# Experts of a mixture-of-experts stage worked in pairs: one transpose of the inner rows for two experts, another order of weight loads and products, ScalarE's gate work behind the feature copies

## The chip, the cores and the metric

The kernel runs on one core of one Trainium2 chip. The metric is the device time of one execution in microseconds (us). A kernel's time is the median of its runs.

## The reference, cut to what matters

An encoder of two layers over 512 tokens of width 1024, in float32. Each layer is a mixer (retention and differential attention in the first, latent attention and gated linear attention in the second), a LayerNorm, a mixture of 32 experts, and another LayerNorm. The change lies in the mixture:

```python
def _hier_moe(x, w_grp, b_grp, w_exp, b_exp, w_gate, w_up, w_down):
    ...
    gate = p_grp[:, None] * jax.nn.softmax(top_l, axis=-1)
    ...
    def expert_block(args):
        idx, e = args
        xb = x_pad[idx]
        hdn = jax.nn.silu(xb @ w_gate[e]) * (xb @ w_up[e])
        return hdn @ w_down[e]
    ...
    out = jnp.zeros((n + 1, d), x.dtype).at[buf_tok].add(y * buf_w[:, None].astype(y.dtype))
```

Every token goes to two of the 32 experts, so all experts are used and all their weights are read: per expert and layer w_gate and w_up of 1024 x 512 and w_down of 512 x 1024, 6 MB, 403 MB over both layers.

## The kernel before, in words

**Weights.** A weight slab is 128 x 2048 float32, 1 MB, and an expert has six: gate and up in two halves each, down in two. `expect_moe` lists the loads in the order in which the products use them; SyncE issues them in that order (line 304), each into a free slot (`slot`, `pump`). A slot is free when TensorE has used its slab. `spare` holds slots back for other tiles.

**Products.** Expert `e` holds up to 64 tokens. Two experts `2p` and `2p+1` make pair `p`: their 128 token rows are fetched from DRAM by GpSimd's indirect DMA (`moe_fetch`, line 1174; below "the gather") to places that `moe_pair` works out on TensorE (4 transposes and 4 small products with `G`) and VectorE (`ridx`). `moe_features` turns these rows with 8 transposes into one PSUM tile, and ScalarE copies it to `xn` (line 1185), two buffers by the pair's parity. `up(e, c)` is half `c` of the gate and up products, 8 products of 64 x 512 (16 matmul instructions in the trace), with `xn` as the stationary operand. After the second half `moe_hidden` makes silu(gate) * up on ScalarE and VectorE (lines 1211 and 1212) in the 64 x 512 tile `h`. `hidden(e)` turns it with 4 transposes of 64 rows and a VectorE copy into `hs`. `down(e)` is 8 products; `moe_gated` (lines 1241, 1242) scales its result by the gate. `sums(p, t)` adds a pair's result to token tile `t`: 4 products with `C` and a VectorE addition (line 1197).

**Order.** In `moe` TensorE's order is the program's. For each expert it is `up(e, 1)`, `down(e-1)`, `up(e+1, 0)`, then `hidden(e)`, and between these `pair` or `features` of a later pair and, at every second expert, the four `sums` of the pair before. A pair's features come at least one expert before the products that read them. The other engines' order comes from a scheduler. Before the first expert stand `moe_features` of pair 0 with two copies, and `moe_gates`, which makes the gate values in `G` (exponentials and a cast on ScalarE). At the end follow `sum_begin`, the last `down`, `sum_end` and the LayerNorm.

Of the kernel before, what the change touches and what calls it, by code (L numbers as in the profile page):

```python
# [11 lines left out]
F32 = mybir.dt.float32  # L12
# [4 lines left out]
AF = mybir.ActivationFunctionType  # L17
OP = mybir.AluOpType
AX = mybir.AxisListType

P = 128
D = 1024
# [7 lines left out]
NE = 32  # L30
NG = 4
EPG = 8
DE = 512
CAP = 64
# [41 lines left out]
class Kernel:  # L76
# [220 lines left out]
    def expect_moe(self, l):  # L297

        I = self.I

        def half(n, e, c):
            j = 4 if n == "moe_w_down" else 8
            wv = I[n][l, e].rearrange("(p j) n -> p j n", j=j)
            self.expect(lambda raw: self.nc.sync.dma_start(
                raw.rearrange("p (j n) -> p j n", j=j // 2), wv[:, c * (j // 2):(c + 1) * (j // 2), :]), local=True)

        def up(e, c):
            half("moe_w_gate", e, c)
            half("moe_w_up", e, c)

        up(0, 0), up(0, 1), up(1, 0)
        for e in range(1, NE + 1):
            if e < NE:
                up(e, 1)
            for c in range(2):
                half("moe_w_down", e - 1, c)
            if e + 1 < NE:
                up(e + 1, 0)

    def new_xT(self):  # L320

# [855 lines left out]
    def moe_features(self, x, xn, parts=1):  # L1177

        xv = x.rearrange("p (k j) -> p j k", j=KJ)
        ps = self.pb()  # L1180
        for j in range(KJ):
            self.tr(ps[:, j * P:(j + 1) * P], xv[:, j, :])
        n = KJ // parts
        for i in range(parts):
            self.nc.scalar.copy(xn[:, i * n:(i + 1) * n], ps[:, i * n * P:(i + 1) * n * P].rearrange("p (j n) -> p j n", j=n))  # L1185
        self.rel(ps)

    def moe_sum(self, m, C, y, ts, first):

# [7 lines left out]
            self.nc.vector.scalar_tensor_tensor(x, x, ALPHA if first else 1.0, ps, op0=OP.mult, op1=OP.add)  # L1197
            self.rel(ps)

    def moe_up(self, o, x, c):  # L1200

        raws = [self.next_raw()[0] for _ in range(2)]
        for j in range(4):
            for i, raw in enumerate(raws):
                self.mm(o[64 * i:64 * i + 64], x[:, 4 * c + j, :], raw[:, j * 512:(j + 1) * 512], c == 0 and j == 0,
                        c == 1 and j == 3)
        self.free(*raws)

    def moe_hidden(self, h, o):

        self.nc.scalar.activation(h, o[0:64], AF.Silu)  # L1211
        self.nc.vector.tensor_tensor(h, o[64:128], h, op=OP.mult)  # L1212
        self.rel(o)

    def moe_hidden_rows(self, r, h):

        hv = h.rearrange("p (k j) -> p j k", j=4)
        ps = self.pa()
        for j in range(4):
            self.tr(ps[:, j * CAP:(j + 1) * CAP], hv[:, j, :], 64)  # L1220
        hs = r.tile([P, 4, CAP], F32, name="hs", bufs=1)
        self.nc.vector.tensor_copy(hs.rearrange("p j n -> p (j n)"), ps[:, 0:4 * CAP])  # L1222
        self.rel(ps)
        return hs

# [20 lines left out]
    def moe(self, m, g, b):  # L1246

        nc, tc, l = self.nc, self.tc, m["layer"]
        self.more_slots(1)
        wst = ExitStack()  # L1250
        r = wst.enter_context(tc.tile_pool(name=f"moe{l}", bufs=1))
        h, C, zs, xs = {}, {}, {}, {}
        LAST = NE // 2 - 1
        hh = r.tile([P, DE], F32, name="h")
        C2 = r.tile([P, 2, T], F32R, name="C")
        m["G"] = r.tile([P, NT, NE // 2, 6], F32R, name="G")
        xbuf, xr, sc = m["xbuf"], m["xr"], m["sc"]
# [2 lines left out]
        def pair(p):  # L1260
            C[p] = last[:, D:D + T] if p == LAST else cz[:, 0:T] if p == LAST - 1 else \
                [sc[:, D:D + T], sc[:, D + T:2 * D], C2[:, 0], C2[:, 1]][p % 4]
            self.moe_pair(m, p, C[p])
            if p + 2 <= LAST:
                self.moe_places(m, p + 2)
            if p > 1:
                self.moe_fetch(m, p)

        def features(p):
            self.moe_features(self.moe_fetched(m, p), xn[:, p % 2])  # L1270

        def parts(t):

            xs[t] = self.slot(F32R)
            self.split(xs[t][:, 0:D], xs[t][:, D:2 * D], self.residual(m, t))
# [27 lines left out]
        y1 = None  # L1303

        def up(e, c):
            if c == 0:
                acc[e] = self.pa()
            self.moe_up(acc[e], xn[:, e // 2 % 2, :, e % 2 * CAP:(e % 2 + 1) * CAP], c)
            if c == 1:
                h[e] = hh[64:128]  # L1310
                self.moe_hidden(h[e], acc.pop(e))

        def hidden(e):
            hs[e] = self.moe_hidden_rows(r, h.pop(e))

        def down(e):
            pd = self.pa() if e < NE - 1 else self.pb()
            for c in range(2):
                self.moe_down(pd, hs[e], c)
            del hs[e]  # L1320
            a, p = 64 * (e % 2), e // 2
            gate = m["gate"][:, p:p + 1]
            if p < LAST:
                z = (yz if p == LAST - 1 else yhl).rearrange("p (k n) -> p k n", k=2)
                self.moe_gated(z[:, 0], z[:, 1], pd, gate, a)
                return
            b_, y1 = 64 - a, last[:, 0:D]
            f, s = slice(b_ * 8, b_ * 8 + 512), slice(a * 8, a * 8 + 512)
            self.after = nc.scalar.activation(y1[a:a + 64, f], pd[b_:b_ + 64, 0:512], AF.Copy, scale=gate[a:a + 64]).ins
            nc.vector.tensor_scalar(y1[a:a + 64, s], pd[a:a + 64, 0:512], gate[a:a + 64], None, op0=OP.mult)  # L1330
            self.rel(pd)

        def sums(p, *ts):
            self.moe_sum(m, C[p], yhl.rearrange("p (k n) -> p k n", k=2), ts, p == 0)

        acc, hs = {}, {}
# [3 lines left out]
        with tc.manual_schedule(engines={mybir.EngineType.PE}):  # L1340
            x = self.moe_fetched(m, 0)
            nc.vector.tensor_copy(x, m["g"])
            self.rel(m.pop("g"))
            self.moe_features(x, xn[:, 0], 2)
            ps = self.pa()
            self.moe_tokens(m, m["S"][:, :, 2:4], self.idr, ps, 1)
            self.rel(ps)
            self.moe_fetch(m, 1, False)
            self.moe_gates(m)
            self.spare = 1  # L1350
            up(0, 0)
            yhl = self.slot(F32R)
            self.spare = 0
            up(0, 1)
            up(1, 0)
            for e in range(NE):
                q, k = divmod(e, 4)
                p = e // 2 - 1
                if e == NE - 10:
                    self.spare = 4  # L1360
                if e == NE - 8:
                    last, cz, yz, gbuf = self.slot(local=False), self.slot(F32R, local=False), self.slot(F32R, local=False), None
                    gbuf = self.load_gb(g, b)
                    self.spare = 0
                    nc.vector.tensor_copy(cz[:, T:T + P], self.eye)
                if e:
                    up(e, 1)
                    down(e - 1)
                    if e + 1 < NE:
                        up(e + 1, 0)  # L1370
                if e == NE - 1:
                    hidden(e)
                    break
                if e == 0:
                    features(1)
                    pair(0), pair(1)
                more = q + 1 < NE // 4
                if k % 2:
                    hidden(e)
                    if more and k == 1:  # L1380
                        pair(2 * q + 3)
                    elif more:
                        features(2 * q + 3)
                    continue
                add = 0 <= p < LAST - 1
                if add:
                    sums(p, 0)
                hidden(e)
                if add:
                    sums(p, 1)  # L1390
                if more and k == 0:
                    pair(2 * q + 2)
                elif more:
                    features(2 * q + 2)
                if add:
                    sums(p, 2, 3)
                if p == LAST - 2:
                    self.spare = 1
                    self.free(sc, yhl)
                    y = yz.rearrange("p (k n) -> p k n", k=2)  # L1400
                    parts(0)
                    self.spare = 2
                if e == NE - 2:
                    self.spare = 0
                    parts(1), parts(2)
            y1 = last[:, 0:D]
            sum_begin(0)
            down(NE - 1)
            sum_begin(1)
            for t in range(3):  # L1410
                sum_end(t)
                if t == 0:
                    sum_begin(2)
# [555 lines left out]
```

## Time and profile before

| | |
|---|---|
| median of 3 runs | 1535.87 us (1528.81, 1535.87, 1539.55) |
| the profiled execution | 1532.13 us; its span from first to last instruction 1530.4 us |
| mean granted clock of TensorE | 0.993 of full speed |
| busy in the span | TensorE 96%, VectorE 47%, ScalarE 28%, GpSimd 9% |
| weight slabs of the experts | 384 loads of 1024 KB, median 18.4 to 19.6 us from issue to landing |
| HBM | 462.11 MB read, 308 GB/s over the span |

The two expert stages lie at about 325 to 785 us and 1050 to 1515 us. A busy TensorE in the profile is not one at its peak, since matmuls are pipelined and their ends are modelled; so pieces of work are measured here from the start of one group of matmuls to the start of the next. In a row, "idle before <- releaser" in square brackets is how long the engine stood before the group and what ended it.

### The profile page before, as it was taken

What the parts mean: (1) busy time and instruction counts of PE and PEld (TensorE: products, weight loads), DVE (VectorE), ACT (ScalarE), POOL (GpSimd) and SP (SyncE); (2) the same over time, 40 slices, a digit from 0 to 9 for tenths busy, and PEclk for the clock granted to TensorE, in tenths of its full rate; (3) what the DMA queues carried; (4) which work ended last, traced back from release to release, by engine and by line L of the source; (5) the groups of instructions that cost most, each with busy time, mean ns of one, the idle gap of its engine ahead of it and who ended that gap; (6) DMA issues with size and microseconds to landing.
All of it is one profiled execution on the core that took longest, in us unless ns stands there. A gap on an engine that the chain in (4) does not pass through costs nothing. (4 is left out here: it accounts for less than half of the span.)

```text
span 1530.4 us, 18251 instructions
## 1 busy us (share of the span) xinstructions
PE 1474.0 (96%) x7057; PEld 840.0 (55%) x7057; DVE 722.6 (47%) x1336; ACT 432.9 (28%) x817; POOL 137.1 (9%) x194
## 2 busy tenths in 40 slices
PE   7999999989999999999999999998999999999997
PEld 6777787854444444444357777684444444444433
DVE  5766858553343343343355744473334334334334
ACT  4655421022112112112246545402221211211222
POOL 0211101120000000010021000111000000001001
PEclk9999999999999999999999999998999999999999
DMA  8211314789999999999962210587999999999993
GB/s 263 65 56 56 108 65 159 270 326 424 426 427 425 426 426 427 425 426 426 427 211 99 83 55 28 209 344 272 407 426 427 425 427 425 427 425 426 426 427 134
DMA packets 105119, 465.02 MB, mean 304 GB/s; under 512 B 13308, under 2 KB 44508, under 8 KB 55744
## 3 DMA queue, kind: packets, MB, share of 16 engines
q1 hardware_dynamic: 97136, 444.86, 71.6%
q0 software_dynamic: 6160, 12.62, 2.4%
q10 hardware_dynamic: 1728, 6.29, 1.0%
q8 instruction: 57, 0.93, 0.2%
q14 instruction: 38, 0.31, 0.1%
HBM read 462.11 MB, written 9.44 MB: 308 GB/s over the span
## 5 line engine op out<-in xcount | busy, mean ns | idle before, releaser
L211 PE MATMUL pa<-big 128*64 128x512 f32 (+2 forms) x3400 | 813.8, 521 | 11.1 <-DMA big<-in_moe_w_up_dram 3.1
L211 PEld LDWEIGHTS pa<-big 128*64 128x64 f32 (+1 forms) x3400 | 397.1, 158 | 345.2 <-issue 272.9
L211 PE MATMUL pa<-big,hs 128*64 128x512 f32 x992 | 224.8, 592 | 0.0
L1242 DVE SCALAR_TENSOR_TENSOR big<-pa,rgate,big 64x512 fp32r<-64x512 f32 x120 | 90.0, 750 | 213.4 <-ACT big L1241 210.5
L211 PE MATMUL pb<-big 128*128 128x512 f32 (+1 forms) x544 | 159.8, 431 | 8.3 <-DVE big L1197 4.2
L1197 DVE SCALAR_TENSOR_TENSOR big<-big,pb 128x1024 f32<-128x1024 f32 x112 | 134.3, 1220 | 69.4 <-PE pb L211 69.1
L211 PEld LDWEIGHTS pa<-big,hs 128*64 128x64 f32 x992 | 72.9, 137 | 140.6 <-issue 134.5
L1212 DVE TENSOR_TENSOR h<-pa,h 64x512 f32<-64x512 f32 x64 | 44.4, 694 | 219.7 <-ACT h L1211 219.7
L1241 ACT ACTIVATE big<-pa,rgate 64x512 fp32r<-64x512 f32 x120 | 81.9, 683 | 218.9 <-PE pa L211 170.2
L211 PEld LDWEIGHTS pb<-big 128*128 128x128 f32 x544 | 98.0, 190 | 54.2 <-issue 25.8
L1211 ACT ACTIVATE h<-pa 64x512 f32<-64x512 f32 x64 | 37.7, 590 | 262.0 <-PE pa L211 262.0
L201 DVE TENSOR_TENSOR big<-big 128x1024 fp32r<-128x1024 f32 (+2 forms) x67 | 80.0, 1207 | 31.6 <-ACT big L201 25.8
L201 ACT CAST big<-big 128x1024 fp32r<-128x1024 f32 (+2 forms) x68 | 68.9, 1044 | 56.0 <-PE pa L211 37.2
L1185 ACT COPY big<-pb 128x1024 f32<-128x1024 f32 (+1 forms) x34 | 32.5, 962 | 118.7 <-PE pb L216 118.7
L1174 POOL DMA_INDIRECT big<-x1d,ridx x30 | 31.4, 1048 | 353.6 <-DVE ridx L1148 232.7
L211 PE MATMUL pb<-big,C 128*128 128x512 f32 x192 | 53.9, 412 | 2.5 <-DVE big L1197 2.5
L216 PEld LDWEIGHTS pa<-eye,h 64*128 64x128 f32 x256 | 35.5, 209 | 37.9 <-DVE big L1242 24.3
L1173 POOL MEMSET big<- 128x1024 f32 x28 | 26.7, 953 | 325.4 <-PE pb L216 325.4
L216 PE MATMUL pb<-eye,big 128*128 128x128 f32 x304 | 43.0, 286 | 8.0 <-DMA big<-in_x_dram 5.0
L1222 DVE COPY hs<-pa 128x256 f32<-128x256 f32 x64 | 27.0, 422 | 43.6 <-PE pa L216 43.5
L216 PEld LDWEIGHTS pb<-eye,big 128*128 128x128 f32 x304 | 38.9, 194 | 14.1 <-issue 11.1
L216 PE MATMUL pa<-eye,h 64*128 64x64 f32 x256 | 44.2, 293 | 0.0
(313 smaller groups left out, 1164.3 us busy)
## 6 DMA issues: line engine op xcount, KB each, us to landing
big<-in_moe_w_gate_dram SPq DMA_DIRECT2D x128, 1024.0 KB, 18.4
big<-in_moe_w_up_dram SPq DMA_DIRECT2D x128, 1024.0 KB, 19.6
big<-in_moe_w_down_dram SPq DMA_DIRECT2D x128, 1024.0 KB, 19.6
big<-in_ev_w_in_dram SPq DMA_DIRECT2D x32, 256.0 KB, 4.8
big<-in_ev_w_in_dram SPq DMA_DIRECT2D x12, 512.0 KB, 5.8
big<-in_od_w_in_dram SPq DMA_DIRECT2D x6, 1024.0 KB, 5.5
big<-in_x_dram SPq DMA_DIRECT2D x8, 512.0 KB, 6.8
big<-in_ev_w_out_dram SPq DMA_DIRECT2D x4, 1024.0 KB, 5.1
```

Source lines behind the costliest of these rows:

```text
L201: ins = self.nc.scalar.copy(hi, src), (sub or self.nc.vector).tensor_tensor(lo, src, hi.bitcast(F32), op=OP.subtract)
L211: return self.nc.tensor.matmul(o, a, b, start=start, stop=stop, skip_group_check=True)
L216: self.nc.tensor.transpose(o, a, self.eye[s, s])
L1173: self.nc.gpsimd.memset(x, 0.0)
L1174: self.nc.gpsimd.indirect_dma_start(x, None, self.x1d[:, :], bass.IndirectOffsetOnAxis(m["idx"][:, pair:pair + 1], 0), bounds_check=T - 1, ...
L1185: self.nc.scalar.copy(xn[:, i * n:(i + 1) * n], ps[:, i * n * P:(i + 1) * n * P].rearrange("p (j n) -> p j n", j=n))
L1197: self.nc.vector.scalar_tensor_tensor(x, x, ALPHA if first else 1.0, ps, op0=OP.mult, op1=OP.add)
L1211: self.nc.scalar.activation(h, o[0:64], AF.Silu)
L1212: self.nc.vector.tensor_tensor(h, o[64:128], h, op=OP.mult)
L1222: self.nc.vector.tensor_copy(hs.rearrange("p j n -> p (j n)"), ps[:, 0:4 * CAP])
L1241: last = self.nc.scalar.activation(hi, src, AF.Copy, scale=g[a:a + 64])
L1242: self.nc.vector.scalar_tensor_tensor(yl[a:a + 64, s], src, g[a:a + 64], hi.bitcast(F32), op0=OP.mult, op1=OP.subtract)
```

## The change

It does five things.
- Loads and products go by pairs: all four halves `up(e+2, ..)`, `up(e+3, ..)` of the next pair lie around the two `down` of this pair, and `expect_moe` lists the slabs in that order.
- The inner rows of both experts stand in one 128 x 512 tile (the free end of the router's tile `y1`, in the place of `h`), and one `hidden(p)` per pair makes 4 transposes of 128 rows and one copy of 512 columns. The odd expert's gate and up halves of PSUM change places for that.
- `features(p + 2)` stands at the end of pair `p`, after `up(e+3, 1)` and straight before `up` of the pair that reads it. `pair(p + 2)` stands after `down(e)`.
- The four `sums` come as two and two, on either side of `up(e+2, 1)`.
- `moe_gates` is issued after the copies of the first features on ScalarE. At the end `hidden` of the last pair and its two `down` follow `sum_begin(0)`.

As `y1` is now in use through the first layer's experts, the loads of the second layer's router weights into a tile of the same place stand behind the last gather in GpSimd's order; before, they stood behind the second.

```diff
-        up(0, 0), up(0, 1), up(1, 0)
-        for e in range(1, NE + 1):
...
+        for e in range(2):
+            up(e, 0), up(e, 1)
+        for e in range(0, NE, 2):
+            if e + 2 < NE:
+                up(e + 2, 0), up(e + 2, 1)
+            for k in range(2):
+                for c in range(2):
+                    half("moe_w_down", e + k, c)
+                if e + 2 < NE:
+                    up(e + 3, k)
...
-    def moe_up(self, o, x, c):
+    def moe_up(self, o, x, c, a):
...
-                self.mm(o[64 * i:64 * i + 64], x[:, 4 * c + j, :], raw[:, j * 512:(j + 1) * 512], c == 0 and j == 0,
+                b = 64 - a if i == 0 else a
+                self.mm(o[b:b + 64], x[:, 4 * c + j, :], raw[:, j * 512:(j + 1) * 512], c == 0 and j == 0,
...
-            self.tr(ps[:, j * CAP:(j + 1) * CAP], hv[:, j, :], 64)
-        hs = r.tile([P, 4, CAP], F32, name="hs", bufs=1)
-        self.nc.vector.tensor_copy(hs.rearrange("p j n -> p (j n)"), ps[:, 0:4 * CAP])
+            self.tr(ps[:, j * P:(j + 1) * P], hv[:, j, :])
+        hs = r.tile([P, 4, P], F32, name="hs", bufs=1)
+        self.nc.vector.tensor_copy(hs.rearrange("p j n -> p (j n)"), ps)
...
-        hh = r.tile([P, DE], F32, name="h")
+        hh = m["y1"][:, D - DE:D]
...
-            self.moe_gates(m)
+            with tc.issue_after(ins):
+                self.moe_gates(m)
...
+            up(1, 0), up(1, 1)
+            features(1)
+            for p in range(LAST):
+                e = 2 * p
...
+                up(e + 2, 0)
+                hidden(p)
+                if p:
+                    sums(p - 1, 0, 1)
+                else:
+                    pair(0)
+                up(e + 2, 1)
+                if p:
+                    sums(p - 1, 2, 3)
...
+                down(e)
+                if p == 0:
+                    pair(1)
+                if p + 2 <= LAST:
+                    pair(p + 2)
+                up(e + 3, 0)
+                down(e + 1)
+                up(e + 3, 1)
+                if p + 2 <= LAST:
+                    features(p + 2)
...
             sum_begin(0)
+            hidden(LAST)
+            down(NE - 2)
             down(NE - 1)
```

TensorE's order in the middle of the first stage, before: `pa<-big` of 64x512 is an `up` half, `pa<-big,hs` a `down`, `pa<-eye,h` the transposes of `hidden`, `pb<-big,C` the `sums`, `pb<-eye,big` the features, `pa<-eye,big` and `pa<-G,big` a `pair`.

```order
L211 MATMUL pa<-big 64x512 x8
L216 MATMUL pa<-eye,h 128x64 x4
L216 MATMUL pa<-eye,big 128x128 x4
L211 MATMUL pa<-G,big 128x6 x4
L211 MATMUL pa<-big 64x512 x8
L211 MATMUL pa<-big,hs 64x512 x8
L211 MATMUL pa<-big 64x512 x8
L211 MATMUL pb<-big,C 128x512 x4
L216 MATMUL pa<-eye,h 128x64 x4
L211 MATMUL pb<-big,C 128x512 x4
L216 MATMUL pb<-eye,big 128x128 x8
L211 MATMUL pb<-big,C 128x512 x8
```

The same engine and place in the changed kernel, a whole pair from features to features, where `pa<-eye,y_111` is the one `hidden` of the pair:

```order
L216 MATMUL pb<-eye,big 128x128 x8
L211 MATMUL pa<-big 64x512 x8
L216 MATMUL pa<-eye,y_111 128x128 x4
L211 MATMUL pb<-big,C 128x512 x8
L211 MATMUL pa<-big 64x512 x8
L211 MATMUL pb<-big,C 128x512 x8
L211 MATMUL pa<-big,hs 64x512 x8
L216 MATMUL pa<-eye,big 128x128 x4
L211 MATMUL pa<-G,big 128x6 x4
L211 MATMUL pa<-big 64x512 x8
L211 MATMUL pa<-big,hs 64x512 x8
L211 MATMUL pa<-big 64x512 x8
```

The features moved to the place just ahead of the `up` half that reads them, and one `hidden` is gone.

TensorE at the end of the second stage, before, from the last `up` half to the last `down` (`pb<-big,hs`), where `pa<-big` of 128x512 is `sum_begin(0)`:

```order
L211 MATMUL pa<-big 64x512 x8
L211 MATMUL pa<-big,hs 64x512 x8
L216 MATMUL pa<-eye,h 128x64 x4
L211 MATMUL pa<-big 128x512 x8
L211 MATMUL pb<-big,hs 64x512 x8
```

The same place in the changed kernel (`y_5143` is the second layer's `y1`):

```order
L211 MATMUL pa<-big 64x512 x8
L211 MATMUL pa<-big 128x512 x8
L216 MATMUL pa<-eye,y_5143 128x128 x4
L211 MATMUL pa<-big,hs 64x512 x8
L211 MATMUL pb<-big,hs 64x512 x8
```

The `sum_begin(0)` that stood between the transposes of `hidden` and a `down` now stands ahead of both.

## Rows read from the trace of the kernel before

**Rows 1.** Busy times in one stretch: PE, PEld, DVE, ACT, POOL, clock, DMA share, GB/s.

```profile
336.00:770.00 434.00, 428.67 (x2057) 189.22 (x2057) 163.89 (x243) 86.17 (x124) 28.15 (x29) 1.00 1.01 425
```

**Rows 2.** TensorE in order of time near the first stage's end: start, us, group.

```profile
730.82 1.02 PE L211 MATMUL pa<-big 128*64 128x512 f32 x2
732.12 3.65 PE L211 MATMUL pa<-big 128*64 128x512 f32 x14 [0.28 <-DMA big<-in_moe_w_up_dram]
...
759.08 1.05 PE L211 MATMUL pa<-big 128*64 128x512 f32 x2
761.54 3.65 PE L211 MATMUL pa<-big 128*64 128x512 f32 x14 [1.42 <-DMA big<-in_moe_w_up_dram]
```

**Rows 3.** TensorE's waits from 320 us on: total us, times, longest.

```profile
PE pb L211 <- DVE big L1197: 6.7, 16, 0.4
PE pa L211 <- DMA big<-in_moe_w_up_dram: 3.1, 3, 1.4
```

**Rows 4.** TensorE in order of time, two experts in the first stage.

```profile
512.05 3.65 PE L211 MATMUL pa<-big 128*64 128x512 f32 x16
515.54 3.60 PE L211 MATMUL pa<-big,hs 128*64 128x512 f32 x16
518.97 3.60 PE L211 MATMUL pa<-big 128*64 128x512 f32 x16
522.50 0.69 PE L216 MATMUL pa<-eye,h 64*128 64x64 f32 x4
...
524.06 3.65 PE L211 MATMUL pa<-big 128*64 128x512 f32 x16
...
534.51 1.20 PE L211 MATMUL pb<-big,C 128*128 128x512 f32 x4
535.64 0.69 PE L216 MATMUL pa<-eye,h 64*128 64x64 f32 x4
536.25 1.20 PE L211 MATMUL pb<-big,C 128*128 128x512 f32 x4
537.29 1.05 PE L216 MATMUL pb<-eye,big 128*128 128x128 f32 x8
538.77 2.10 PE L211 MATMUL pb<-big,C 128*128 128x512 f32 x8 [0.42 <-DVE big L1197]
540.80 3.65 PE L211 MATMUL pa<-big 128*64 128x512 f32 x16
```

**Rows 5.** All engines in order of time, first features of the first stage.

```profile
323.97 1.14 PE L216 MATMUL pb<-eye,big 128*128 128x128 f32 x8 [1.47 <-DVEq L1338]
...
325.14 1.07 ACT L1185 COPY big<-pb 128x512 f32<-128x512 f32 x2 [0.64 <-PE pb L216]
...
325.78 10.59 PE L211 MATMUL pa<-big 128*64 128x512 f32 x48 [0.33 <-ACT big L1185]
```

**Rows 6.** Groups by line, 330 to 775 us: busy us, mean ns of one, idle before.

```profile
L1185 ACT COPY big<-pb 128x1024 f32<-128x1024 f32 x15 | 15.2, 1013 | 59.0 <-PE pb L216 59.0
L1222 DVE COPY hs<-pa 128x256 f32<-128x256 f32 x32 | 13.5, 422 | 21.8 <-PE pa L216 21.8
```

**Rows 7.** A gather in order of time.

```profile
525.09 1.04 POOL L1174 DMA_INDIRECT big<-x1d,ridx  x1 [12.56 <-issue]
```

**Rows 8.** The line of the gathers (L1174): time from issue to landing, all 30.

```profile
DMA to landing us min/median/max: 3.4/8.2/9.3
```

**Rows 9.** All engines in order of time, first features of the second stage.

```profile
1047.13 1.14 PE L216 MATMUL pb<-eye,big 128*128 128x128 f32 x8 [1.47 <-DVEq L1338]
...
1049.61 0.30 ACT L201 CAST G<-y 128x128 fp32r<-128x128 f32 x1 [1.95 <-DVE ridx L1148]
1049.81 1.07 ACT L1185 COPY big<-pb 128x512 f32<-128x512 f32 x2
...
1050.44 13.02 PE L211 MATMUL pa<-big 128*64 128x512 f32 x48 [1.84 <-ACT big L1185]
```

**Rows 10.** What the DMA engines moved, GB/s in 40 slices of 1 us from 1040 us.

```profile
GB/s 418 426 229 16 0 33 82 221 377 344 33 41 123 0 0 16 0 82 213 410 377 164 279 442 410 434 426 434 410 434 434 361 221 164 336 369 418 418 410 434
```

More of the change, by code (lines that the diff above doesn't have):

```diff
@@ L309, in up @@
             half("moe_w_up", e, c)
-        up(0, 0), up(0, 1), up(1, 0)
-        for e in range(1, NE + 1):
[L313 to L318, printed above, removed]
+        for e in range(2):
[8 more added lines that the diff above has]
+                    up(e + 3, k)
     def new_xT(self):
@@ L1184, in moe_features @@
         for i in range(parts):
-            self.nc.scalar.copy(xn[:, i * n:(i + 1) * n], ps[:, i * n * P:(i + 1) * n * P].rearrange("p (j n) -> p j n", j=n))
+            ins = self.nc.scalar.copy(xn[:, i * n:(i + 1) * n], ps[:, i * n * P:(i + 1) * n * P].rearrange("p (j n) -> p j n", j=n)).ins
         self.rel(ps)
+        return ins
     def moe_sum(self, m, C, y, ts, first):
@@ L1204, in moe_up, with moe_hidden @@
             for i, raw in enumerate(raws):
-                self.mm(o[64 * i:64 * i + 64], x[:, 4 * c + j, :], raw[:, j * 512:(j + 1) * 512], c == 0 and j == 0,
+                b = 64 - a if i == 0 else a
+                self.mm(o[b:b + 64], x[:, 4 * c + j, :], raw[:, j * 512:(j + 1) * 512], c == 0 and j == 0,
                         c == 1 and j == 3)
         self.free(*raws)
-    def moe_hidden(self, h, o):
-        self.nc.scalar.activation(h, o[0:64], AF.Silu)
-        self.nc.vector.tensor_tensor(h, o[64:128], h, op=OP.mult)
+    def moe_hidden(self, h, o, a):
+        h = h[a:a + 64]
+        self.nc.scalar.activation(h, o[64 - a:128 - a], AF.Silu)
+        self.nc.vector.tensor_tensor(h, o[a:a + 64], h, op=OP.mult)
         self.rel(o)
@@ L1307, in up, with hidden @@
                 acc[e] = self.pa()
-            self.moe_up(acc[e], xn[:, e // 2 % 2, :, e % 2 * CAP:(e % 2 + 1) * CAP], c)
+            self.moe_up(acc[e], xn[:, e // 2 % 2, :, e % 2 * CAP:(e % 2 + 1) * CAP], c, e % 2 * CAP)
             if c == 1:
[L1310 to L1314, printed above, removed]
+                self.moe_hidden(hh, acc.pop(e), e % 2 * CAP)
+        def hidden(p):
+            hs[p] = self.moe_hidden_rows(r, hh)
         def down(e):
+            a, p = 64 * (e % 2), e // 2
             pd = self.pa() if e < NE - 1 else self.pb()
             for c in range(2):
-                self.moe_down(pd, hs[e], c)
-            del hs[e]
-            a, p = 64 * (e % 2), e // 2
+                self.moe_down(pd, hs[p][:, :, a:a + 64], c)
             gate = m["gate"][:, p:p + 1]
@@ L1343, in moe @@
             self.rel(m.pop("g"))
-            self.moe_features(x, xn[:, 0], 2)
+            ins = self.moe_features(x, xn[:, 0], 2)
             ps = self.pa()
@@ L1354, in moe @@
             up(0, 1)
[L1355 to L1359, printed above, removed]
+            up(1, 0), up(1, 1)
+            features(1)
+            for p in range(LAST):
+                e = 2 * p
+                if p == 11:
                     self.spare = 4
-                if e == NE - 8:
+                if p == 12:
                     last, cz, yz, gbuf = self.slot(local=False), self.slot(F32R, local=False), self.slot(F32R, local=False), None
@@ L1365, in moe @@
                     nc.vector.tensor_copy(cz[:, T:T + P], self.eye)
[L1366 to L1397, printed above, removed]
+                up(e + 2, 0)
[7 more added lines that the diff above has]
+                    sums(p - 1, 2, 3)
+                if p == LAST - 1:
                     self.spare = 1
@@ L1402, in moe @@
                     self.spare = 2
-                if e == NE - 2:
-                    self.spare = 0
-                    parts(1), parts(2)
+                down(e)
[8 more added lines that the diff above has]
+                    features(p + 2)
+            self.spare = 0
+            parts(1), parts(2)
             y1 = last[:, 0:D]
             sum_begin(0)
+            hidden(LAST)
+            down(NE - 2)
             down(NE - 1)
```

## The prediction, made before the changed kernel ran

> **What bounds the kernel now.** I read the page's slices first, then the busy times of the stretch between the first and the last expert, then TensorE in order of time inside it and at its two ends, and last ScalarE and the DMA around the start of each stage. In the stretch the DMA share is 1.01 at 425 GB/s and TensorE is busy 428.67 of 434 us [rows 1], so both look like the bound. TensorE's waits tell them apart. From 320 us to the end it waits for a weight slab only three times, 3.1 us in total [rows 3], and in the first stage only near its end [rows 2]. So for most of the stage TensorE trails the DMA: slabs were loaded ahead while it still worked on the mixer, and it draws nearer all the time. One pair of experts costs it 28.75 us, from 512.05 to 540.80 [rows 4]. The DMA needs 12 slabs of 1.049 MB at 425 GB/s, 29.6 us, and more with the gather. TensorE therefore gains about 1 us and a half per pair and meets the DMA near 730 us. There two matmuls that take 0.43 us elsewhere (16 in 3.43, from 515.54 to 518.97 [rows 4]) stretch to 1.30 and 2.46 [rows 2], so TensorE loses 0.87 and 2.03 us, together 2.9 us. That is all the slack: TensorE may become 2.9 us slower over a whole stage before the end of the stage moves, and if it becomes faster it only meets the DMA earlier.
>
> **What each part costs TensorE, over one stage of 16 pairs.**
>
> Inner rows: 32 groups of 4 transposes go, 0.61 us each from 535.64 to 536.25 [rows 4], 19.5 us. 16 groups of 4 transposes of 128 rows come. Eight such transposes take 1.06 us (537.29 to 538.77 less a wait of 0.42 [rows 4]); four are 0.53, with the change of tile shape about 0.55, and no more than the old 0.61. That is 8.8 us. Gain 10.7.
>
> Sums: two blocks of 4 and one of 8 cost 1.13, 1.04 and 2.03 (534.51 to 535.64, 536.25 to 537.29, 538.77 to 540.80), 4.20; two blocks of 8 cost 4.06. Over 14 pairs this gains 2.0. The wait for VectorE's addition, 0.42 us and 8 times in a stage (16 in both [rows 3]), goes too, since an `up` half of 3.4 us now stands between the two blocks: gain 3.4.
>
> Shape changes: an `up` or `down` in the middle of a run costs 3.43, the first of a run 3.49 and the last 3.53 [rows 4]. Two runs of three become one run of three and three single groups, 0.32 us more per pair, 4.8 in 15.
>
> Features: this is the new wait. Until now a pair's features were an expert ahead; now the `up` that reads them is the next thing in TensorE's order. At the start of the stage the trace shows this very sequence: transposes at 323.97, ScalarE's copy from 325.14, `up` at 325.78, 0.11 after the first half of the copy [rows 5]. In the loop the copy is one piece of 1.013 us [rows 6], so `up` starts 1.17 + 1.01 + 0.11 = 2.29 us after the first transpose instead of 1.06. The stall is 1.23 us, 15 times, 18.4 us. Behind the waiting `up` stand `hidden`, the sums and the next `down`, all in order, so nothing fills it. ScalarE's silu of the expert before needs 0.6 us and is done while the transposes run.
>
> Sum per stage: 18.4 + 4.8 - 10.7 - 2.0 - 3.4 = 7.1 us slower on TensorE. From both sides: were the stall only the copy (1.0) and the four transposes 0.41, it would be 1.3; were the transposes no cheaper and single groups all 0.1 dearer, 10.
>
> End of the stage: the work behind the last `up` half is the same, but `down(30)` now waits for the copy of `hs`. Before, `sum_begin(0)` covered it. The copy of 256 columns takes 0.422 us [rows 6]; 512 columns I put at 0.7, with the way there and back a stall of 0.9 us (0.5 to 1.2).
>
> Start: in the first stage the feature copies follow the transposes at once [rows 5], so moving the gate work gives nothing. In the second stage ScalarE first waits for VectorE with the cast of `G`: the copies start at 1049.81 though the transposes, begun at 1047.13, took 1.14, and TensorE stands 1.84 us [rows 9]. Moved behind, the copies start about 1.5 us earlier. The clock is at 1.2 GHz there after TensorE's pauses (48 matmuls take 13.02 against 10.59 us in the first stage [rows 5, 9]), so 0.8 to 1.5 of it is left; I take 1.1.
>
> DMA: the second stage's DMA stops between 1044 and 1060, and once more it falls, to 221, 164, 336 and 369 GB/s in four slices [rows 10], 1.4 us lost against 426, because no slot came free while TensorE did pairs instead of products. The new order frees eight slabs in one go, and this hole closes. It is worth something only if the DMA sets the end. The router loads that move on GpSimd cost nothing: it is busy 28 of 434 us [rows 1] and their reader is a mixer away; I allow 0 to 2 us for what they take from the DMA at the layer boundary.
>
> **The sum.** First stage 7.1 - 2.9 + 0.9 = 5.1. Second stage, with the same slack (its one large wait is the third of the 3.1 us in rows 3), 5.1 - 1.1 = 4.0. Together 9.1, against the profiled execution's 1532.13: 1541.2. That execution lies 3.7 below the median of the three runs and within their range, so its time is a fair base; I predict 1541.5.
>
> **Rivals.**
>
> *The DMA covers it.* If TensorE's loss stays below the slack, the end hangs on the last slab: 0 in the first stage, -1.1 - 1.4 in the second, plus 0.9 twice for the tails: 1531.4, or 1529.6 if the tails are free. For it speaks the DMA share of 1.01 [rows 1]; against it that TensorE is late for most of the stage and the slack is only 2.9 [rows 2]. It needs a loss of 2.9 or less where I count 7.1 and bound it at 1.3 below. The Trainium skill (Perfetto Trace Analysis, Identifying the Most-Contended Engine) says that gains come from the most contended engine; by it only the DMA would count here and the time would be this rival's. The trace agrees that the DMA is full, but shows TensorE behind it for 400 us.
>
> *Late gather, slower.* The rows of pair p+2 are now asked for in the same pair in which they are transposed. In the trace a gather starts 1.03 us after the next `up` (525.09 and 524.06 [rows 4, 7]). The features follow that `up` after three groups, 10.45 us (512.05 to 522.50 [rows 4]), so it has 9.42 us; it lands after 8.2 in the median and 9.3 at most [rows 8]. That fits by 1.2 and 0.1 us. If `ridx` stands 2.5 us longer on VectorE, behind the additions of `down(e)`, TensorE waits 1.3 us in each of 14 pairs of both stages, 36 us: 1577. It decides once the gather starts 1.2 us later. In the new order `ridx` stands ahead of those additions, which speaks against it.
>
> *The pair's transposes are not cheaper.* If four of 128 rows ran one after another at 0.28 each, `hidden` would cost 1.1 instead of 0.55, 8.8 more per stage: 1558.8. The features' eight in 1.06 us [rows 4] speak against it. The Trainium skill (TensorE: Matmul & The Clock Gate, Part 4: PE-mode transpose) gives about 275 ns for a 128 x 128 transpose inside a kernel, which would make it this; the trace shows 0.13 us each when they follow one another.
>
> **How the numbers follow.** TensorE's loss beyond the slack (forecast) 0.57, the DMA covers it 0.28, late gather 0.10, dear transposes 0.05. The range must leave out no more than 2 in 10: from just under the second case with the runs' own spread, 1528, to beyond the dear transposes, 1562. The forecast alone spans 1533 to 1549. One per cent, about what a measurement of this kernel can tell from no change, is 15.4 us: slower than 1551 are late gather, dear transposes and little else, 0.14; faster than 1520 has no mechanism here but an error of mine, 0.03; within it 0.83.
>
> **What would show it.** In the new profile: a wait of TensorE for ScalarE's feature copy (line 1187) of 1.0 to 1.3 us about 30 times, and a pair of experts at about 29.0 us, waits included; 0.55 us from `hidden` to the next group; no waits for VectorE's additions; the gate cast behind the copies in the second stage and its first products some 1.5 us nearer the transposes; no or smaller waits for slabs near 760 us. If waits for slabs remain at both ends, the DMA covered the loss and I am wrong by the second case. A wait of the features' transposes for a gather would show the third.

## The result and the profile after

The changed kernel takes 1544.85 us (median of 8 runs, 1541.51 to 1550.57), the kernel before 1537.44 in 8 runs beside it: ratio 1.0058, 95% interval 1.0032 to 1.0085. That is 9 us slower by the ratio and 7.4 by the medians, small, though the interval leaves out 1, and within the one per cent that the prediction called "no change". 1541.5 was forecast.

The profiled run took 1541.51 us, the shortest of the eight, its span 1539.7, 9.3 more than before. I read first the busy times of the first stage (columns as in [rows 1]), then TensorE's waits from 320 to 1515 us.

```profile
336.00:780.00 444.00, 424.21 (x2009) 178.99 (x2005) 158.92 (x229) 85.37 (x125) 27.64 (x29) 1.00 1.01 422
```

```profile
PE pa L211 <- ACT big L1187: 33.7, 32, 1.1
PE pa L211 <- DVE big L1247: 4.3, 2, 2.2
...
PE pa L216 <- DVE y L1217: 2.2, 2, 1.1
...
PE pa L211 <- issue: 1.7, 2, 0.8
```

The DMA share is still 1.01, but TensorE is now idle for 19.8 of 444 us where it was idle for 5.3 of 434 [rows 1]. It no longer waits for a slab at all: the row of [rows 3] is gone, and so is VectorE's addition. In its place stands the feature copy, 32 times: 30 in the loop at 1.1 us and one short wait at the start of each stage. Three more come once in a stage: for line 1247 (4.3 us in both stages), for 1217 (2.2) and "issue" (1.7). Only the last was foreseen.

The DMA in 40 slices of 1 us from 1480 us, GB/s:

```profile
GB/s 434 442 426 401 434 451 418 410 418 451 418 410 426 434 410 418 377 385 360 311 180 156 41 0 0 0 0 0 0 0 0 0 0 0 0 0 0 0 0 0
```

The last slab lands at about 1502.5 us; the last `down` of the changed kernel starts at 1512.01. TensorE ends the stage some 9 us behind the DMA. In the kernel before the transfers end as early, and its last `down` starts at 1502.64, level with them:

```profile
GB/s 442 401 426 434 442 426 418 418 418 434 426 418 426 434 410 410 352 377 262 172 123 74 16 0 0 0 0 0 0 0 0 0 0 0 0 397 127 0 0 94
```

TensorE in order of time, one steady pair, answering to [rows 4]:

```profile
517.10 1.17 PE L216 MATMUL pb<-eye,big 128*128 128x128 f32 x8
519.36 3.65 PE L211 MATMUL pa<-big 128*64 128x512 f32 x16 [1.10 <-ACT big L1187]
522.95 0.75 PE L216 MATMUL pa<-eye,y 128*128 128x128 f32 x4
523.45 2.09 PE L211 MATMUL pb<-big 128*128 128x512 f32 x8
...
548.32 1.08 PE L211 MATMUL pa<-big 128*64 128x512 f32 x4 [1.10 <-ACT big L1187]
```

A pair takes 28.96 us (519.36 to 548.32; forecast about 29.0, before 28.75). The pair's `hidden` costs 0.50 (forecast 0.55), and `up` starts 2.26 us after the first feature transpose (forecast 2.29).

The first of the two not foreseen, at pair 0 of the first stage. TensorE, then VectorE, then the clock (busy times of the stretch, the clock ahead of the DMA share):

```profile
355.94 0.66 PE L216 MATMUL pa<-eye,big 128*128 128x128 f32 x4
356.35 0.59 PE L211 MATMUL pa<-G,big 128*128 128x6 f32 x4
356.80 0.66 PE L216 MATMUL pa<-eye,big 128*128 128x128 f32 x4
359.62 0.61 PE L211 MATMUL pa<-G,big 128*128 128x6 f32 x4 [2.17 <-DVE big L1247]
360.16 5.35 PE L211 MATMUL pa<-big 128*64 128x512 f32 x16
```

```profile
357.19 0.74 DVE L1247 SCALAR_TENSOR_TENSOR big<-pa,rgate,big 64x512 fp32r<-64x512 f32 x1
357.96 0.17 DVE L1165 TENSOR_REDUCE rgate<-pa 64x1 f32<-64x2 f32 x1
358.14 0.69 DVE L1142 TENSOR_TENSOR big<-io,rpos 128x512 fp32r<-128x512 f32 x1
358.82 0.75 DVE L1247 SCALAR_TENSOR_TENSOR big<-pa,rgate,big 64x512 fp32r<-64x512 f32 x1
```

```profile
361.30:364.60 3.30, 3.30 (x10) 0.96 (x8) 0.09 (x1) 0.00 (x0) 0.97 (x1) 0.50 1.00 422
```

At p = 0 two `pair` follow the first `down`, in later pairs one. The second runs out of `pa` tiles of PSUM: the `down`'s tile is held until line 1247 has gated its second half, behind the first pair's own VectorE work, at 359.57. Right behind this wait the clock is at 0.50 (1.2 GHz), and the `up` half takes 5.18 us (to the next start, 365.34) instead of 3.49. Both recur in the second stage (1086.75: wait 2.17; the next half 5.18). That is 2.17 + 1.7 = 3.9 us a stage.

The other stands at the end of a stage, beside the foreseen one. TensorE from the last `up` half on (16 matmuls, merged with the 8 of `sum_begin(0)`), then VectorE:

```profile
773.12 5.64 PE L211 MATMUL pa<-big 128*64 128x512 f32 x24
779.85 0.75 PE L216 MATMUL pa<-eye,y 128*128 128x128 f32 x4 [1.09 <-DVE y L1217]
781.43 3.65 PE L211 MATMUL pa<-big,hs 128*64 128x512 f32 x16 [0.83 <-issue]
784.88 3.63 PE L211 MATMUL pb<-big,hs 128*64 128x512 f32 x16
```

```profile
777.84 1.23 DVE L201 TENSOR_TENSOR big<-big 128x1024 fp32r<-128x1024 f32 x1 [1.53 <-ACT big L201]
779.10 0.70 DVE L1217 TENSOR_TENSOR y<-pa,y 64x512 f32<-64x512 f32 x1
780.63 0.69 DVE L1227 COPY hs<-pa 128x512 f32<-128x512 f32 x1 [0.84 <-PE pa L216]
```

The 0.83 us is the copy of `hs`, as forecast (0.9). The 1.09 us is new: the split of a residual block (`parts`; its cast stands ahead of the silu on ScalarE, its subtraction ahead of line 1217 here) delays the last hidden values.

The start of the second stage, answering to [rows 9]:

```profile
1052.99 1.12 PE L216 MATMUL pb<-eye,big 128*128 128x128 f32 x8 [1.47 <-DVEq L1341]
...
1054.78 7.58 PE L211 MATMUL pa<-big 128*64 128x512 f32 x34 [0.33 <-ACT big L1187]
```

The wait of 1.84 is now 0.33, so the gate work is out of the way. What the DMA moved, 40 slices of 1 us from 1040, answering to [rows 10]:

```profile
GB/s 410 434 418 418 418 434 426 426 418 426 213 57 0 8 147 270 418 328 49 147 229 401 344 188 360 459 401 434 410 459 401 434 410 459 418 418 418 426 426 434
```

The late fall of [rows 10], 221 to 369 GB/s in four slices from 1072 us, is gone.

A gather of the steady pair on GpSimd, and the time to landing of all 30:

```profile
536.64 1.00 POOL L1176 DMA_INDIRECT big<-x1d,ridx  x1 [17.36 <-DVE big L1247]
```

```profile
DMA to landing us min/median/max: 3.5/8.1/9.1
```

It starts 9.42 us ahead of the features that need it (546.06), and TensorE waits for none.

### The profile page after: what moved, and what is told of

It reads as the page before. It is cut to its first block, busy times and chain, and to the rows that moved or that the text cites. A ratio compares the mean times of both kernels' runs of the same rounds, so it can differ in the third digit from the quotient of the medians.

```text
span 1539.7 us, 18112 instructions
## 1 busy us (share of the span) xinstructions
PE 1454.6 (94%) x6929; PEld 815.1 (53%) x6929; DVE 711.3 (46%) x1304; ACT 430.0 (28%) x817; POOL 136.1 (9%) x194
## 5 line engine op out<-in xcount | busy, mean ns | idle before, releaser
L211 PE MATMUL pb<-big 128*128 128x512 f32 (+1 forms) x544 | 154.7, 427 | 4.2 <-DVE big L1098 3.1
L211 PEld LDWEIGHTS pa<-big,hs 128*64 128x64 f32 x992 | 69.0, 137 | 136.1 <-issue 132.8
L1216 ACT ACTIVATE y<-pa 64x512 f32<-64x512 f32 x64 | 37.9, 592 | 326.0 <-PE pa L211 325.9
L1217 DVE TENSOR_TENSOR y<-pa,y 64x512 f32<-64x512 f32 x64 | 44.1, 689 | 131.0 <-ACT y L1216 130.9
L1227 DVE COPY hs<-pa 128x512 f32<-128x512 f32 x32 | 22.1, 692 | 157.0 <-PE pa L216 157.0
L211 PE MATMUL pb<-big,C 128*128 128x512 f32 x192 | 50.3, 404 | 0.0
L1150 DVE TENSOR_SCALAR ridx<-pa 128x1 int32<-128x1 f32 x34 | 5.4, 158 | 86.7 <-PE pa L211 86.5
L211 PEld LDWEIGHTS pb<-big,C 128*128 128x128 f32 x192 | 34.4, 189 | 16.0 <-issue 9.7
L216 PEld LDWEIGHTS pa<-eye,big 128*128 128x128 f32 x208 | 24.2, 161 | 30.8 <-issue 23.2
```

The lines of the kernel that those rows point to most:

```text
L211: return self.nc.tensor.matmul(o, a, b, start=start, stop=stop, skip_group_check=True)
L216: self.nc.tensor.transpose(o, a, self.eye[s, s])
L1216: self.nc.scalar.activation(h, o[64 - a:128 - a], AF.Silu)
L1217: self.nc.vector.tensor_tensor(h, o[a:a + 64], h, op=OP.mult)
```

## The experiments

Theory T: TensorE sets the end of a stage, and what the change adds to its waits is the loss. R1: the new order of the slabs, that is the DMA, sets the length. R2: the loss is in stretches at 1.2 GHz and in the start and end of a stage. The table has every run. "Stage" is read as above, from the start of the first `up` to the start of the last `down` in the profile (after: 327.66 to 784.88 and 1054.78 to 1512.01). Low clock also falls into a stage or between stages where no edit explains it: a kernel's runs differ by 1.0 to 1.6 us for each 0.001 of mean granted clock. So the last column is the time that a straight line through a kernel's own runs, over their mean clock, gives at 0.993; that is an estimate, and a short extrapolation for e7_more; e6_double_copy had no run near that clock.

| kernel | median us | ratio to before (95% interval) | stage 1 | stage 2 | at clock 0.993 |
|---|---|---|---|---|---|
| before | 1533.94 to 1537.44 | 1 | 450.31 | 452.20 | 1532.9 |
| after | 1544.85 | 1.0058 (1.0032 to 1.0085) | 457.22 | 457.23 | 1543.2 |
| e1_cover | 1526.73 | 0.9948 (0.993 to 0.9967) | 449.85 | 449.42 | 1529.1 |
| e2_halves | 1531.79 | 0.9989 (0.9968 to 1.0009) | 450.81 | 450.84 | 1531.0 |
| e6_double_copy | 1597.41 | 1.0407 (1.0386 to 1.0427) | 484.12 | 480.97 | (0.977 to 0.980) |
| e4_p0 | 1540.18 | 1.0026 (1.0013 to 1.0038) | 454.69 | 454.93 | 1538.8 |
| e5_tail | 1548.39 | 1.0076 (1.0058 to 1.0094) | 458.16 | 459.65 | 1545.0 |
| e5b_tail | 1543.53 | 1.0055 (1.0035 to 1.0075) | 455.58 | 455.61 | 1540.3 |
| e10_p0_tail | 1534.89 | 1.0003 (0.9986 to 1.002) | 451.59 | 451.65 | 1535.5 |
| e7_more | 1564.19 | 1.0194 (1.0168 to 1.0221) | 462.77 | 462.80 | 1554.9 |
| e3_gates | 1532.80 | 0.9994 (0.998 to 1.0009) | 451.76 | 449.30 | 1532.4 |
| e8_best | 1527.55 | 0.9944 (0.9926 to 0.9961) | 450.49 | 448.26 | 1527.2 |

**Work over the feature copy (e1_cover, from the changed kernel).**

```diff
+                if p:
+                    sums(p - 1, 0, 1)
+                else:
+                    pair(0)
                 up(e + 2, 0)
                 hidden(p)
-                if p:
-                    sums(p - 1, 0, 1)
-                else:
-                    pair(0)
                 up(e + 2, 1)
```

> The sums of two blocks (at the first pair the placing of pair 0) are moved ahead of the up half that follows the features; nothing else. Theory T (TensorE sets the end, and the wait for the feature copy is its largest loss): the 1.10 us in front of that up half, 15 times a stage, goes; a steady pair falls from 28.96 to about 27.9 us, TensorE gains 16.5 us a stage, meets the DMA again before the end (in the changed kernel the slabs were all there 9.4 us before the last down began), waits for slabs come back, and the program is 12 to 18 us faster than the changed kernel, so 3 to 10 under the kernel before. Rival R1 (the new order of the slabs, that is the DMA, sets the length of a stage): the pair gets shorter but slab waits take its place, within 4 us of the changed kernel. Rival R2 (the loss is the 1.2 GHz windows and the two new waits at the first pair and at the tail): within 4 us of the changed kernel, and no slab waits.

TensorE in order of time over the feature copy, and its largest waits from 320 to 1515 us:

```profile
537.42 1.16 PE L216 MATMUL pb<-eye,big 128*128 128x128 f32 x8
538.34 1.18 PE L211 MATMUL pb<-big,C 128*128 128x512 f32 x4
539.69 1.20 PE L211 MATMUL pb<-big,C 128*128 128x512 f32 x4 [0.17 <-ACT big L1187]
540.82 3.65 PE L211 MATMUL pa<-big 128*64 128x512 f32 x16
```

```profile
PE pa L211 <- DMA big<-in_moe_w_up_dram: 4.7, 4, 1.9
PE pb L211 <- ACT big L1187: 4.6, 28, 0.2
```

The 1.10 us are gone, a pair takes 28.24 us (512.58 to 540.82), TensorE waits for slabs again, and the program is 18 us faster than the changed kernel (14 at equal clock), 8 under the kernel before. T had this; neither R1 nor R2 allows more than 4. The pair fell by 0.7 and not by 1.1: these sums take 2.48 us (538.34 to 540.82) for 2.02, 0.17 of it a wait for the feature copy, and `hidden` costs 0.67 for 0.50.

**The copy in halves (e2_halves, from the changed kernel).**

```diff
-            self.moe_features(self.moe_fetched(m, p), xn[:, p % 2])
+            self.moe_features(self.moe_fetched(m, p), xn[:, p % 2], 2)
```

> The changed kernel with the feature copy of every pair in two halves, so that the up half behind it may begin after the first. T: the wait falls from 1.10 to about 0.35 us (what the same two halves leave at the start of a stage), 15 times: 11 us of TensorE a stage, of which the last part meets the DMA; 6 to 8 us a stage, 12 to 16 in all under the changed kernel, so 3 to 7 under the kernel before. R1 (the order of the slabs): no change.

```profile
516.67 1.17 PE L216 MATMUL pb<-eye,big 128*128 128x128 f32 x8
518.51 3.65 PE L211 MATMUL pa<-big 128*64 128x512 f32 x16 [0.67 <-ACT big L1187]
```

The wait fell to 0.67, not 0.35: at the start of a stage four small products (326.74) stand between transposes and `up` and hide the rest. From the transposes to `up` it is 1.81 us there and 1.84 here. 15 x 0.43 = 6.5 us a stage; the stages lost 6.4. No slab wait came, so all of it counted. By the ratios 10.6 us came off, a little under the 12 to 16 expected, for the same reason.

**The copy twice (e6_double_copy, from the changed kernel).**

```diff
-            ins = self.nc.scalar.copy(...).ins
+            for _ in range(3 - parts):
+                ins = self.nc.scalar.copy(...).ins
```

> In the loop ScalarE copies a pair's features twice to the same place (the values are the same), so the up half behind it waits one copy longer. T: the wait grows from 1.10 to about 2.1 us, 15 times a stage with nothing over it: 15 us a stage, 28 to 32 us in all over the changed kernel. R1: TensorE has 9 us a stage to give, so 10 to 14 us in all. R2: as T.

TensorE at two pairs, and the busy times and clock of 370 us of the first stage:

```profile
499.44 3.65 PE L211 MATMUL pa<-big 128*64 128x512 f32 x16 [2.15 <-ACT big L1188]
...
529.44 5.17 PE L211 MATMUL pa<-big 128*64 128x512 f32 x16 [2.15 <-ACT big L1188]
```

```profile
400.00:770.00 370.00, 344.24 (x1588) 143.40 (x1586) 125.94 (x179) 77.30 (x109) 23.68 (x25) 0.97 0.99 408
```

It cost 53 us by medians, 20 more than T said, and R1's 10 to 14 are far off. The wait is 2.15 as expected, 15.8 us a stage more. The rest is the clock: behind some of these waits the half takes 5.1 to 5.3 us to the next start, and in these 370 us the mean clock is 0.97 (1.00 in the changed kernel). 3% of 370 us lost at half speed is 22 us at 1.2 GHz, which cost 11. The stages grew by 26.9 and 23.7: wait and clock together are 27 in the first, and in the second five halves of 5.1 to 5.3 us stand behind such waits.

**One placing behind the first `down` (e4_p0, from the changed kernel).**

```diff
-                    pair(0)
+                    pair(0), pair(1)
...
-                if p == 0:
-                    pair(1)
```

> The placing of pair 1 is moved from behind the first down to where pair 0 is placed, so that only one placing follows the first down, as in every later pair. T and R2: the 2.17 us in which TensorE waits for a PSUM tile that the first down's gating still holds goes, and with it the fall of the granted clock right behind it (1.7 us): up to 3.9 us a stage, 4 to 8 us in all under the changed kernel; if the fall of the clock has another cause and stays, 4.3 in all. R1: no change.

TensorE behind the first `down`:

```profile
364.17 0.59 PE L211 MATMUL pa<-G,big 128*128 128x6 f32 x4
364.69 3.65 PE L211 MATMUL pa<-big 128*64 128x512 f32 x16
```

The wait and the slow half behind it are gone, and 4.9 us come off by the ratios. The profiled stages are only 2.5 and 2.3 us shorter, since each has 1.2 GHz at another place: the first 64 matmuls take 15.5 us for 14.0 in e1_cover, and the second stage's `down` at 1510.23 takes 5.15 for 3.43.

**The tail (e5_tail, e5b_tail, from the changed kernel).** `up` now returns the VectorE product of `moe_hidden` as `ins`, and `sum_begin` can make one of its halves.

```diff
-            parts(1), parts(2)
+            with tc.issue_after(ins):
+                parts(1), parts(2)
             y1 = last[:, 0:D]
-            sum_begin(0)
+            sum_begin(0, (0,))
             hidden(LAST)
+            sum_begin(0, (1,))
```

> At the end of a stage the splitting of residual blocks 1 and 2 is issued behind the last product of hidden values, and the products of the last sum that stand ahead are cut in two halves, one ahead of the last transposes and one between them and the down that reads them. T and R2: the 1.09 us in front of the last hidden transposes and the 0.83 us in front of the down go, less 0.1 to 0.2 for one more change of shape: 1.7 us a stage, 3 to 4 us in all under the changed kernel. R1: no change, for the tail then waits for the slab of the last down.

It did not help: the stages are 0.9 and 2.4 us longer. The time is some 3 us longer by the ratios, within the intervals. VectorE, then TensorE:

```profile
781.94 0.69 DVE L1217 TENSOR_TENSOR y<-pa,y 64x512 f32<-64x512 f32 x1 [2.14 <-ACT y L1216]
782.67 2.36 DVE L201 TENSOR_TENSOR big<-big 128x1024 fp32r<-128x1024 f32 x2
785.06 0.69 DVE L1228 COPY hs<-pa 128x512 f32<-128x512 f32 x1
```

```profile
785.86 3.65 PE L211 MATMUL pa<-big,hs 128*64 128x512 f32 x16 [1.49 <-issue]
```

Now both subtractions, 2.36 us, stand ahead of the copy of `hs`, and a cast still stood ahead of the silu. The second edit sets each behind an instruction of its own engine (`ins` is now the silu, `self.copied` the copy of `hs`):

```diff
             sum_begin(0, (0,))
             hidden(LAST)
+            with tc.issue_after(ins):
+                for t in (1, 2):
+                    xs[t] = self.slot(F32R)
+                    nc.scalar.copy(xs[t][:, 0:D], self.residual(m, t))
+            with tc.issue_after(self.copied):
+                for t in (1, 2):
+                    nc.vector.tensor_tensor(xs[t][:, D:2 * D], ...)
             sum_begin(0, (1,))
```

> As the tail experiment before, but the two casts stand behind the last silu on ScalarE and the two subtractions behind the copy of the last inner rows on VectorE (there they had come ahead of that copy, and the down waited 1.49 in place of 0.83 us). T: the two tail waits, 1.92 us together, fall to about 0.4: 1.4 us a stage, 2 to 4 us in all under the changed kernel. R1: no change.

```profile
783.58 0.75 PE L216 MATMUL pa<-eye,y 128*128 128x128 f32 x4 [0.29 <-DVE y L1217]
784.09 1.17 PE L211 MATMUL pa<-big 128*128 128x512 f32 x4
785.19 3.65 PE L211 MATMUL pa<-big,hs 128*64 128x512 f32 x16
```

The waits fall from 1.92 to 0.29, and both stages are 1.6 shorter. The median alone does not show it (1.0055 against 1.0058, intervals of 0.004); at equal clock it is 2.9 us.

**Both unforeseen waits out (e10_p0_tail):** the edits of e4_p0 and e5b_tail together.

> The two waits that were not foreseen are both taken out (one placing behind the first down, the mended tail), and the wait for the feature copy is left. T: 4.0 and 1.6 us a stage by the traces of the two single edits, 11 us in all under the changed kernel, within 4 us of the kernel before; TensorE stays late and no slab wait comes. Rival: the waits overlap with the DMA after all, and less than 5 us comes off.

Both stages are 5.6 us shorter than in the changed kernel, 3.9 + 1.6 with nothing lost, and the program is level with the kernel before (1.0003), the feature wait still being there. So R2 has its share: these two waits, with the slow half behind one, are as large as the whole net loss. The feature wait costs TensorE more (1.10 us, 15 times a stage), but what the change gains elsewhere pays for most of it.

**TensorE work added to the kernel before (e7_more).**

```diff
-            self.tr(ps[:, j * CAP:(j + 1) * CAP], hv[:, j, :], 64)
+            for _ in range(2):
+                self.tr(ps[:, j * CAP:(j + 1) * CAP], hv[:, j, :], 64)
```

> The kernel before with every inner-row transpose done twice (same values to the same place), 128 more transposes of 64 rows in a stage, about 0.4 us per expert by the old group of four at 0.61, so 13 us more of TensorE a stage. T: the kernel before has only its slab waits of 3 to 4 us a stage to give, so the end moves by 9 to 10 us a stage, 16 to 22 us in all over the kernel before. R1 (the DMA sets the stage and TensorE has room): 0 to 5 us.

The group of eight takes 1.10 us (517.82 to 518.92) for 0.61 [rows 4], so 15.7 us a stage and not 13. The stages grew by 12.5 and 10.6, one half of the first at 1.2 GHz costing 1.7 us (344.44: 5.18 us for 3.49), and no slab wait is left; R1 is out for the kernel before too. In the first stage 15.7 - (12.5 - 1.7) = 4.9 us of slack were used up. By medians it cost 30 us, 8 more than the upper end expected; at equal clock 22.

**The gate order alone, in the kernel before (e3_gates).** `ins` is the last feature copy.

```diff
-            self.moe_gates(m)
+            with tc.issue_after(ins):
+                self.moe_gates(m)
```

> The kernel before with one part of the change alone: ScalarE's and VectorE's gate work is queued behind the first features. T: the second stage's first products start 1.5 us after the transposes' end sooner (wait 1.84 to about 0.33 us), but the kernel before meets the DMA in every stage, so the end keeps to the last slab: 0 to 1.5 us under the kernel before, not measurable. R2 (the start of the stages counts in full, with the clock): 2 to 5 us under it.

The wait at the start of the second stage fell as in the changed kernel, slab waits remained (4.0 us in three), and the time did not change measurably (0.998 to 1.0009).

**Together (e8_best):** the edits of e1_cover (with `pair(0), pair(1)` in the place of `pair(0)`), e4_p0 and e5b_tail.

> Three edits together: the sums of two blocks (at the first pair both placings) over the feature copy, one placing behind the first down, and this tail. T: the first alone brought TensorE back to waiting for slabs, so the second adds nothing to the time but the third does, since the tail comes after the last slab: 1 to 1.5 us a stage under that kernel, 1522 to 1526 us, 10 to 14 under the kernel before. Rival: the tail's waits are filled by the last slabs anyway, and the time is that kernel's within 1 us.

1527.55 us, 0.9944 of the kernel before and level with e1_cover by medians (0.9948; at equal clock 1.9 us under it). The 1522 to 1526 of T were not reached by the median, and the 1.9 us are too little to tell T from the rival. Slab waits are 8.8 us in seven now: the DMA sets the stage, and further savings on TensorE ahead of the last slab are not seen in the time.

## Why the prediction was right, and where not

The mechanism held: TensorE is the engine that ends a stage, the feature copy is its new wait, and covering it (e1), halving it (e2) or doubling it (e6) moves the time by what TensorE gains or loses, until the slabs are late. That the total, 9.1 forecast and 9.3 in the profile, came so near is luck: errors cancelled between the terms, and the 9.3 is 1.9 ahead of the first stage (granted clock 0.98 from 160 us to the first `up`, 1.00 in the kernel before), 6.9 and 5.0 in the stages, -4.5 between them and -0.1 behind. By terms, per stage:

- *Slack 2.9: 4.5. This step failed.* The two stalls of [rows 2] were measured on the two matmuls that stretched, 0.87 and 2.03. The 14 behind them also took 3.58 us for 3.10 (start to next start; both halves are the last of a run, 3.53), so the halves lost 1.35 and 2.51, and a third stall was left out:

```profile
769.23 0.59 PE L211 MATMUL pa<-big,hs 128*64 128x512 f32 x1
769.48 0.59 PE L211 MATMUL pa<-big 128*64 128x512 f32 x1
769.66 3.85 PE L211 MATMUL pa<-big,hs 128*64 128x512 f32 x15
```

In the kernel before a `down`, again the last of its run, and the last matmul of an `up` lose 0.67 there (0.25 + 3.77 less 3.53, and 0.18). e7's 4.9 is near it.
- *TensorE's loss in the pairs, 7.1: about 5.6.* e10 is 1.3 us longer than before in the first stage, 0.3 of it tail; 1.0 + 4.5 is the loss. By the rows of a steady pair it is 18.0 + 4.8 - 11.7 - 2.0 - 3.4 = 5.7. The feature step is right: 2.26 us for 1.06, 1.20 a pair where I took 1.23. So are the shape changes (the six halves of a pair take 21.22 us for 20.90, the 0.32 forecast) and the sums without VectorE's waits. Most of the difference, 1.0, lies in the inner rows: 0.50 us for four where I took 0.55.
- *Tail 0.9: 1.9. "The work behind the last `up` half is the same" failed.* It looked at TensorE's order alone. On ScalarE and VectorE the splitting of a residual block had come ahead of the last hidden values, 1.09 us.
- *Pair 0: nothing forecast, 3.9 measured.* I followed the steady pair and never the first, where two `pair` come in a row and the PSUM tiles run out. e4 shows the wait of 2.17. The 1.7 at low clock goes with it there, but e1 has the wait without them.
- Sum: 5.6 - 4.5 + 1.9 + 3.9 = 6.9; the first stage grew by 6.9. Forecast was 5.1. The second grew by 5.0, but in the kernel before it had 2.4 us of low clock at its first products (13.02 for 10.59 us [rows 5, 9]).
- *Start of the second stage, -1.1.* The wait went as forecast (1.84 to 0.33). Between the stages (last `down` to first `up`) 274.35 us became 269.90, but before had 1.2 GHz there and at the second stage's first products, so the share of the gate order can't be read from these two profiles. e3 says that alone it is worth nothing that can be measured, as the slabs then end the stage.
- *The DMA's hole* closed as forecast, and counts for nothing while TensorE ends 9 us behind.

Of the rivals, "the DMA covers it" is out: no slab wait was left. It came back only where TensorE was made faster, in e1 and e8. The Trainium skill (Perfetto Trace Analysis, Identifying the Most-Contended Engine) takes the engine of highest occupancy, for the DMA the HBM utilization, as the one to optimize first. Here the busy share of the DMA engines was 1.01 in both kernels and the stage still moved with TensorE's waits, so that share alone would not have shown the loss. The late gather did not come: it had the 9.42 us worked out, against 9.1 at most to land. The dear transposes neither: 0.50 us for four. The Trainium skill (TensorE: Matmul & The Clock Gate, Part 4: PE-mode transpose) gives about 275 ns for one in a kernel, by which an estimate for four is 1.1 us; the trace decides.

Open: whether the 8 us of e1 under the kernel before are all its own. Its stages are only 0.5 us shorter than those of before where no low clock lies in them, its runs had a mean clock of 0.9946 against 0.9914, and at equal clock 3.8 us remain. Whether the edit or chance raised the clock was not tried.

## What to carry to other kernels

A share of 1.01 on one engine does not make it the bound: look whose waits end last, and how much slack the other has over the whole stage. When a producer is moved next to its consumer, the copy between them is paid at every turn; put two or three short groups between them, here 18 us by medians and 14 at equal clock. And cost the first and last turn of a loop apart from the steady one, on every engine: there 5.6 us a stage lay, of the 6.9 that the first stage grew.

## What was not expected of the hardware

- Behind a short wait the clock can fall, and then more is lost than the wait. After the 2.17 us wait at pair 0 the granted clock was at 1.2 GHz in both stages of the changed kernel, 1.7 us more each; over the first stage, with its 15 waits of 1.10 us, the mean clock is 1.00 in the row above. With waits of 2.15 us it fell behind some, not all: 499.44 ran at full speed, 529.44 did not. The 2.17 us wait at pair 0 stands in six kernels; in five a slow half followed it in both stages, in e1_cover in neither (356.97; the next half 3.48). And in e7_more, which has no such wait, the half at 344.44 was slow all the same (5.18). So that the wait causes the fall is not shown, and what decides it was not isolated.
- Low clock also stands where no edit explains it, in other places from kernel to kernel (ahead of the first stage in the changed kernel, between the stages in the kernel before). A kernel's own runs differ with it by several us: 1541.51 at 0.993 and 1550.57 at 0.989 in the changed one. That is the size of most effects here, and only the stage lengths and the granted clock beside the times set them apart.
